# Attention in jobs of four query blocks, with products over up to 512 queries and one buffer for each row of probabilities

## The chip, the cores and the metric

The kernel runs on one core of a Trainium2 chip. The metric is the device time of one execution in microseconds (us), given as the median of several runs. The core has five engines with queues of their own: TensorE (PE in the profile, with its weight loads PEld apart), VectorE (DVE), ScalarE (ACT), GpSimd (POOL), and SyncE (SP), which here only issues DMAs. Each works through its queue in the order of the program; semaphores make one wait for another.

## The reference, cut to what matters

One encoder layer over 1024 tokens and a width of 1024, in float32. Half of the mixer is attention with 8 heads of width 64, in which every query sees itself and the keys ahead of it, and a decay `c` is added to the logits; the other half is a pooling mixer. An output projection, a gated feed-forward layer and a norm follow.

```
for i in range(S // Q_BLOCK):                      # 8 blocks of 128 queries
    q0, q1 = i * Q_BLOCK, (i + 1) * Q_BLOCK
    logits = einsum('bhqd,bhkd->bhqk', qf[:, :, q0:q1], kf[:, :, :q1])
    logits = logits + c[:, :, q0:q1, None] - c[:, :, None, :q1]
    logits = where(s_pos <= t_pos, logits, -inf)
    p = softmax(logits, axis=-1)
    outs.append(einsum('bhqk,bhkd->bhqd', p, vf[:, :, :q1]))
...
x = x + einsum('bse,ed->bsd', concat([attn, pool]), w_out)
x = x + einsum('bsf,fd->bsd', silu(gate) * up, w_down)
```

## The kernel before, in words

Float32 products are made from halves: a matrix is split into a rounded high part and the remainder, and one product becomes three matmuls (`mm3`, lines 157 to 159). The split itself is a copy on ScalarE (line 117) and a subtraction on VectorE or GpSimd (line 118).

The program has three long stages: the norm of the input with the first projections; the attention of the four pairs of heads; then the output projection's rest, the feed-forward layer and the last norm. The change touches the attention alone.

`scores(h, i)` makes a **row of probabilities**, that is the 128 queries of block i of head h against the (i+1)*128 keys that they see. TensorE writes the logits in chunks of up to 512 keys (tile `z`, lines 502 and 503, three PSUM banks in turn). VectorE moves each chunk to the row's tile `p` and takes a minimum (line 505), ScalarE takes the exponent over the whole row (line 511), VectorE the reciprocal of the sum (line 513), and GpSimd scales the row (line 514). Only then may it be transposed.

`turn` transposes a piece of up to four 128x128 blocks of such rows (tile `tp`, line 527, two banks in turn), ScalarE copies it to `th` (line 531) and VectorE makes the remainder `tl` (line 532). `values` multiplies the values of a key block with `th` and `tl` into the bank `po` (line 541), of which there is one. `combine` adds the two halves of `po` (ScalarE's `tmp`, line 552, and VectorE's `at`, line 553) and stores the result to DRAM (tile `mixd`, line 554, an SP queue issue).

A **job** before is a head with a super block `sb` of two query blocks. It has sb+1 pieces; a piece holds two key blocks for the two query blocks, so a product has 256 queries, or 128 where only the second block sees the keys. While a job is turned and multiplied, the rows of the next job are scored. `attend(p, fill, counts)` runs the eight jobs of a pair of heads, and puts steps of other work (`fill`) between: `project` for queries and keys of the next pair (tile `qk`), `project_v23` (tile `v`), and for the last pair the output projection of the chunks that are done (`first_rows` and `second_rows`, tiles `o4`, `o6`, which read the pages `mix` and `wo`). `counts` gives each job its number of fill steps.

This is the order in which the code is written. A scheduler then lays out each engine's queue by when it believes operands to be ready, so that rows of different jobs and fill mix.

Tags set the buffers: the rows 2k and 2k+1 share a tag with two buffers, so there is one buffer for each of a head's eight rows, and a row's logits can be moved by VectorE only when the last transposition of the same row of the head before has run.

After the last job, the last chunk of the mixer's output (`mix3`) is read back from DRAM in two halves (`mix_halves`, lines 749 and 117, 118), while the rest of the fill runs; then `last_row` uses it.

## Time and profile before

| what | value |
|---|---|
| time, median of 3 runs | 1048.54 us (1048.2 to 1049.61) |
| the profiled execution's own time | 1049.96 us |
| its span, first to last instruction | 1048.2 us |
| mean granted TensorE clock | 0.996 |
| first transposition of attention probabilities | 124.5 us after the start |
| last product of probabilities and values | 359.5 us |
| DMA, mean rate over the span | 125 GB/s |

The durations of matmuls in the profile have modelled ends and overlap: a matmul with 512 columns is listed with 0.39 us, yet the next one starts much earlier. How long TensorE is taken by a matmul is therefore read from the start of one to the start of the next. Where such a distance is longer than usual, TensorE stood still, even if the view of waits, which counts from the modelled end, shows less or nothing. For the other engines the listed duration is used.

### The profile page before, as it was taken

To read this page: it belongs to the slowest core of one execution; us is meant where nothing else is said; L and a number is where in the kernel's file an instruction comes from. 1 tells how busy PE (TensorE), PEld (TensorE's weight loads), DVE (VectorE), ACT (ScalarE), POOL (GpSimd) and SP (SyncE) were. 2 spreads that over 40 slices of the span, in tenths; PEclk is the share of its full clock that TensorE was granted. 3 is DMA by queue.
4 is the path that set the end of the run, shared out by engine and by line. 5 is a ranking of instruction groups with operands and counts; after the bars stand their busy time and mean duration, and the time that the engine had idled before them with its cause. 6 is when DMAs were issued, how large, how long until landed. Compare 5 with 4: busy or idle time off the path is not lost.

```text
span 1048.2 us, 14193 instructions
## 1 busy us (share of the span) xinstructions
PE 1031.0 (98%) x5104; PEld 871.5 (83%) x5104; DVE 631.0 (60%) x993; ACT 455.5 (43%) x730; POOL 379.9 (36%) x310
## 2 busy tenths in 40 slices
PE   8999999999999999999999999999999999999996
PEld 7988888998888888888888888888888888888885
DVE  5645466666687569753343434334334689788886
ACT  6434364665556347533333333333233343333345
POOL 4350122114237034267347437437537510000044
PEclk9999999999999999999999999999999999999998
DMA  8114434333733125333234143143146755352424
GB/s 272 47 42 127 106 96 99 83 83 96 258 117 107 53 101 181 91 111 116 85 102 140 61 133 118 61 131 111 63 128 236 248 210 174 119 189 92 155 87 160
DMA packets 109462, 130.73 MB, mean 125 GB/s; under 512 B 8272, under 2 KB 71248, under 8 KB 109392
## 3 DMA queue, kind: packets, MB, share of 16 engines
q1 hardware_dynamic: 97952, 108.71, 33.3%
q10 hardware_dynamic: 11088, 20.45, 5.1%
q8 instruction: 40, 0.66, 0.2%
q0 software_dynamic: 352, 0.66, 0.2%
q14 instruction: 30, 0.25, 0.1%
HBM read 86.81 MB, written 33.03 MB: 114 GB/s over the span
## 4 chain that ended last, share of the span: by engine, by line
PE 92%; DVE 2%; issue 2%; DMA 2%; POOL 1%; ACT 1%; POOLq 0%; SPq 0%; DVEq 0%; ACTq 0%
PE gu_P L158 13%; PE gu_P L159 13%; PE gu_P L157 13%; PE d L158 6%; PE d L157 6%; PE d L159 6%; PE po L541 3%; PE tp L527 3%; PE qk L157 3%; PE qk L158 3%; PE o L157 3%; PE o L158 3%; PE qk L159 3%; PE o L159 2%; PE z L503 1%
## 5 line engine op out<-in xcount | busy, mean ns | idle before, releaser
L118 DVE TENSOR_TENSOR gu_P_l<-s,gu_P_h 128x1024 fp32r<-128x1024 f32 (+1 forms) x48 | 66.3, 1389 | 98.3 <-ACT gu_P_h L117 93.4
L158 PE MATMUL d<-d,d 128*128 128x512 f32 x308 | 119.9, 389 | 0.0
L159 PE MATMUL d<-d,d 128*128 128x512 f32 x308 | 119.9, 389 | 0.0
L514 POOL TENSOR_SCALAR p<-p,rr 128x128 f32<-128x128 f32 (+3 forms) x64 | 47.6, 749 | 182.1 <-DVE rr L513 152.0
L157 PE MATMUL d<-d,d 128*128 128x512 f32 x308 | 108.2, 389 | 0.0
L117 ACT ACTIVATE d<-r_f 128x1536 fp32r<-128x1536 f32 (+1 forms) x28 | 38.7, 1383 | 117.6 <-PE d L158 105.3
L118 DVE TENSOR_TENSOR gu_P_l<-r,gu_P_h 128x1024 fp32r<-128x1024 f32 x32 | 48.5, 1516 | 64.7 <-ACT gu_P_h L117 64.7
L946 POOL TENSOR_TENSOR s<-r 128x1024 f32<-128x1024 f32 x10 | 24.0, 2398 | 162.9 <-DMA r<-in_w_up_dram 103.1
L117 ACT ACTIVATE gu_P_h<-r 128x1024 fp32r<-128x1024 f32 x32 | 33.9, 1061 | 92.0 <-PE gu_P L158 31.6
L158 PEld LDWEIGHTS d<-d,d 128*128 128x128 f32 x308 | 57.8, 188 | 12.1 <-DVE d L118 0.2
L157 PEld LDWEIGHTS d<-d,d 128*128 128x128 f32 x308 | 57.8, 188 | 12.1
L159 PEld LDWEIGHTS d<-d,d 128*128 128x128 f32 x308 | 57.8, 188 | 12.0
L1169 POOL TENSOR_SCALAR sse<-sse 128x1 f32<-128x1 f32 x8 | 5.2, 646 | 158.2 <-ACT junk L1168 158.2
L511 ACT ACTIVATE p<-p,mn 128x128 f32<-128x128 f32 (+3 forms) x64 | 49.4, 773 | 24.8 <-DVE mn L505 22.2
L532 DVE TENSOR_TENSOR tl<-tp,th 128x512 fp32r<-128x512 f32 (+1 forms) x80 | 49.9, 632 | 16.8 <-ACT th L531 16.5
L531 ACT ACTIVATE th<-tp 128x512 fp32r<-128x512 f32 (+1 forms) x80 | 43.2, 552 | 31.6 <-PE tp L527 20.0
L1033 POOL TENSOR_TENSOR h<-h,qh 128x512 f32<-128x512 f32 x33 | 44.4, 1347 | 31.9 <-ACT qh L1031 23.2
L117 ACT ACTIVATE gu_P_h<-s 128x1024 fp32r<-128x1024 f32 (+1 forms) x48 | 47.0, 984 | 19.1 <-PE gu_P L158 12.1
L1030 DVE TENSOR_TENSOR qh<-gu_P,sn_sU 128x512 f32<-128x512 f32 x22 | 15.2, 690 | 61.1 <-POOL h L1033 32.9
L118 DVE TENSOR_TENSOR d<-r_f,d 128x1536 fp32r<-128x1536 f32 (+1 forms) x28 | 45.6, 1628 | 10.3 <-ACT d L117 10.3
L157 PE MATMUL qk<-hTh,h_qk 128*128 128x512 f32 x128 | 50.3, 393 | 0.9 <-ACT th L531 0.9
L158 PE MATMUL qk<-hTl,h_qk 128*128 128x512 f32 x128 | 50.5, 395 | 0.0
(309 smaller groups left out, 3082.0 us busy)
## 6 DMA issues: line engine op xcount, KB each, us to landing
r_f<-hsdP SPq DMA_DIRECT2D x77, 256.0 KB
r_wd<-in_w_down_dram SPq DMA_DIRECT2D x22, 512.0 KB
hsdP<-f ACTq DMA_DIRECT2D x43, 256.0 KB
r<-in_w_gate_dram SPq DMA_DIRECT2D x21, 512.0 KB
r<-in_w_up_dram SPq DMA_DIRECT2D x21, 512.0 KB
s<-hi SPq DMA_DIRECT2D x64, 128.0 KB
hsdP<-h ACTq DMA_DIRECT2D x32, 256.0 KB
x<-in_x_dram SPq DMA_DIRECT2D x8, 512.0 KB
```

The costliest lines, as they stand in the source:

```text
L117: mark["hi"] = nc.scalar.activation(out=hi, in_=src, func=AF.Copy)
L118: return eng.tensor_tensor(out=lo, in0=src, in1=f32(hi), op=ALU.subtract)
L157: nc.tensor.matmul(ps, lh, rh, start=start, stop=False, **kw)
L158: nc.tensor.matmul(ps, lh, rl, start=False, stop=False, **kw)
L159: mark["mm"] = nc.tensor.matmul(ps, ll, rh, start=False, stop=stop, **kw)
L511: nc.scalar.activation(out=pr[:, :n], in_=pr[:, :n], func=AF.Exp, scale=-1.0, bias=mn, accum_out=rs)
L514: nc.gpsimd.tensor_scalar(out=pr[:, :n], in0=pr[:, :n], scalar1=rr, scalar2=1.0, op0=ALU.mult, op1=ALU.mult)
L527: nc.tensor.transpose(tp[:, w : w + P], probs[h, 2 * sb + a][:, s * P : (s + 1) * P], ident)
L531: nc.scalar.activation(out=th[:, :w], in_=tp[:, :w], func=AF.Copy)
L532: nc.vector.tensor_tensor(out=tl[:, :w], in0=tp[:, :w], in1=f32(th[:, :w]), op=ALU.subtract)
L541: mark["pv"] = nc.tensor.matmul(po[:, first * P : 2 * P], vt[p][:, s, j, :], part[:, o : o + wd], start=(s == 0 and part is th), stop=(s = ...
L1033: nc.gpsimd.tensor_tensor(out=h, in0=h, in1=q, op=ALU.mult)
```

## The change

A job is now a head with four query blocks (r0 = 0 or 4), so there are 16 jobs in place of 32. A piece is one key block for all of the job's query blocks that see it; the last two of the four diagonal key blocks that are narrow share a piece as told in `pieces`. A head has ten pieces before and after, with the same 36 transposed blocks. Products now have 512, 384, 256 or 128 queries. All four rows of the next job are scored during a job, and the first four rows of the first head at the start. `combine` runs 16 times over 512 queries in place of 32 times over 256, and `tmp` has one buffer in place of two. Each row of probabilities has a tag and one buffer of its own size. The counts of fill steps of two old jobs are summed; in the last pair they are 29 in place of 27 of 32 steps, so that 3 steps in place of 5 are left behind the last job.

```
-        pr = ap_.tile([P, (2 * (i // 2) + 2) * P], F32, tag=f"pr{i // 2}", bufs=2, name=f"p{h}_{i}")
+        pr = ap_.tile([P, n], F32, tag=f"pr{i}", bufs=1, name=f"p{h}_{i}")
...
+    def pieces(r0):
+
+        return [(s,) for s in range(r0 + 1)] + [(r0 + 1, r0 + 3), (r0 + 2,)]
...
-        for s in (2 * pc, 2 * pc + 1):
-            first = 0 if s <= 2 * sb else 1
+        for s in pieces(r0)[pc]:
+            first = max(0, s - r0)
             spans.append((s, w, first))
-            for a in range(first, 2):
-                nc.tensor.transpose(tp[:, w : w + P], probs[h, 2 * sb + a][:, s * P : (s + 1) * P], ident)
+            for a in range(first, nr):
+                nc.tensor.transpose(tp[:, w : w + P], probs[h, r0 + a][:, s * P : (s + 1) * P], ident)
...
-            wd = (2 - first) * P
+            wd = (nr - first) * P
             for part in (th, tl):
                 mark["pv"] = nc.tensor.matmul(
-                    po[:, first * P : 2 * P], vt[p][:, s, j, :], part[:, o : o + wd],
-                    start=(s == 0 and part is th), stop=(s == 2 * sb + 1 and part is tl),
+                    po[:, first * P : nr * P], vt[p][:, s, j, :], part[:, o : o + wd],
+                    start=(s == 0 and part is th), stop=(s == end and part is tl),
                 )
...
-        tmp = ap_.tile([P, 256], F32, tag="tmp", bufs=2, name=f"tmp{h}_{sb}")
-        at = ap_.tile([P, 256], F32, tag="at", bufs=2, name=f"at{h}_{sb}")
-        nc.scalar.activation(out=tmp[mine, :], in_=po[other, 0:256], func=AF.Copy)
-        nc.vector.tensor_tensor(out=at[mine, :], in0=po[mine, 0:256], in1=tmp[mine, :], op=ALU.add)
-        nc.sync.dma_start(out=mixd[p, mine, sb * 256 : (sb + 1) * 256], in_=at[mine, :])
+        w = nr * P
+        tmp = ap_.tile([P, 512], F32, tag="tmp", bufs=1, name=f"tmp{h}_{r0}")
+        at = ap_.tile([P, 512], F32, tag="at", bufs=2, name=f"at{h}_{r0}")
+        nc.scalar.activation(out=tmp[mine, :w], in_=po[other, :w], func=AF.Copy)
+        nc.vector.tensor_tensor(out=at[mine, :w], in0=po[mine, :w], in1=tmp[mine, :w], op=ALU.add)
+        nc.sync.dma_start(out=mixd[p, mine, r0 * P : r0 * P + w], in_=at[mine, :w])
...
-    jobs = [(h, sb) for h in range(H) for sb in range(NSB)]
+    jobs = [(h, r0, 4) for h in range(H) for r0 in (0, 4)]
...
-    attend(0, project(1), [5, 4, 4, 3, 8, 6, 6, 0])
-    attend(1, both(project(2), project_v23()), [10, 7, 6, 8, 10, 8, 12, 0])
+    attend(0, project(1), [9, 7, 14, 6])
+    attend(1, both(project(2), project_v23()), [17, 14, 18, 12])
...
-    attend(2, project(3, first_chunk), [5, 2, 1, 6, 14, 7, 7, 1])
+    attend(2, project(3, first_chunk), [7, 7, 21, 8])
...
-    attend(3, fill, [3, 3, 4, 4, 4, 4, 3, 2], drain=False)
+    attend(3, fill, [6, 8, 7, 8], drain=False)
```

The order of every queue between the first transposition and the last product changes with it; before and behind that stretch TensorE's queue holds the same rows in the same order. Three places follow. In names like `tp1_0_1`, the first number is the head, the second the job (sb before, r0 now), the third the piece; `z1_7_512` is head 1, row 7, the chunk from key 512; `p1_2` is head 1, row 2.

**Place 1**, TensorE where head 0 ends and head 1 begins. Before, behind the logits of head 1's row 7:

```order
L502 MATMUL z1_7_512_1789<-s1_1_0_1_1131,s1_0_0_1_1023 128x512
L503 MATMUL z1_7_512_1789<-s2_1_0_1_1133,s2_0_0_1_1025 128x512
L502 MATMUL z2_0_0_1831<-s1_1_1_0_1576,s1_0_1_0_1245 128x128
L503 MATMUL z2_0_0_1831<-s2_1_1_0_1578,s2_0_1_0_1247 128x128
L158 MATMUL qk0_2_1_1990<-hTl_106,h_qk0_2_1910 128x512
L541 MATMUL po0_3_1470<-tl0_3_3_1539,v0_174 128x256
L541 MATMUL po0_3_1470<-th0_3_3_1538,v0_174 128x128
L541 MATMUL po0_3_1470<-tl0_3_3_1539,v0_174 128x128
L527 MATMUL tp1_1_0_1648<-ident_62,p1_2_1589 128x128
L527 MATMUL tp1_1_0_1648<-ident_62,p1_3_1606 128x128
```

The same place on TensorE now:

```order
L502 MATMUL z1_7_512_1694<-s1_1_0_1_1131,s1_0_0_1_1023 128x512
L503 MATMUL z1_7_512_1694<-s2_1_0_1_1133,s2_0_0_1_1025 128x512
L546 MATMUL po0_4_1404<-tl0_4_6_1532,v0_174 128x256
L531 MATMUL tp1_0_1_1625<-ident_62,p1_1_1439 128x128
L531 MATMUL tp1_0_1_1625<-ident_62,p1_2_1464 128x128
L531 MATMUL tp1_0_1_1625<-ident_62,p1_3_1492 128x128 x2
L502 MATMUL z2_0_0_1734<-s1_1_1_0_1571,s1_0_1_0_1268 128x128
L503 MATMUL z2_0_0_1734<-s2_1_1_0_1573,s2_0_1_0_1270 128x128
L502 MATMUL z2_1_0_1759<-s1_1_1_0_1571,s1_0_1_0_1268 128x256
L503 MATMUL z2_1_0_1759<-s2_1_1_0_1573,s2_0_1_0_1270 128x256
L531 MATMUL tp1_0_2_1670<-ident_62,p1_2_1464 128x128
L531 MATMUL tp1_0_2_1670<-ident_62,p1_3_1492 128x128
```

Row 7 of head 1 is scored when that head's own first job is being turned, and no `qk` matmul stands between it and its first transposition, which comes 35 matmuls later (`tp1_4_0<-p1_7`); before, its first transposition stood 110 matmuls behind it, 48 of them `qk`.

**Place 2**, ScalarE where head 4 ends, with the pages of the output projection's first chunks (`h_mix6`, `h_wo7`). Before:

```order
L531 ACTIVATE th4_3_3_3125<-tp4_3_3_3121 128x384
L117 ACTIVATE h_mix6_3681<-r_mix6_3564 128x1024
L531 ACTIVATE th5_0_0_3153<-tp5_0_0_3149 128x384
L511 ACTIVATE p5_6_3363,rs5_6_3374<-p5_6_3363,mn5_6_512_3372 128x896
L117 ACTIVATE h_wo7_3741<-r_wo7_3566 128x1024
L552 ACTIVATE tmp4_3_3140<-po4_3_3050 64x256
```

ScalarE there now:

```order
L117 ACTIVATE h_wo5_3417<-r_wo5_3410 128x1024
L535 ACTIVATE th4_4_4_2986<-tp4_4_4_2981 128x512
L535 ACTIVATE th4_4_5_3000<-tp4_4_5_2995 128x512
L511 ACTIVATE p5_4_3054,rs5_4_3065<-p5_4_3054,mn5_4_512_3063 128x640
L535 ACTIVATE th4_4_6_3009<-tp4_4_6_3006 128x256
L117 ACTIVATE h_mix6_3537<-r_mix6_3424 128x1024
L511 ACTIVATE p5_5_3100,rs5_5_3111<-p5_5_3100,mn5_5_512_3109 128x768
L535 ACTIVATE th5_0_0_3036<-tp5_0_0_3031 128x512
L117 ACTIVATE h_wo7_3590<-r_wo7_3426 128x1024
L511 ACTIVATE p5_6_3151,rs5_6_3162<-p5_6_3151,mn5_6_512_3160 128x896
L558 ACTIVATE tmp4_4_3022<-po4_4_2873 64x512
```

One exponent more (`p5_5`) stands between the page `h_mix6` and the copy `tmp` that frees the bank `po` for head 5, and `h_wo5` now stands between the pieces of head 4's long job.

**Place 3**, VectorE where head 5 ends and the second round of output rows (`o6`) begins. Before:

```order
L532 TENSOR_TENSOR tl6_0_0_3536<-tp6_0_0_3531,th6_0_0_3535 128x384
L513 RECIPROCAL rr6_7_3788<-rs6_7_3786 128x1
L553 TENSOR_TENSOR at5_3_3504<-po5_3_3429,tmp5_3_3503 64x256
L695 TENSOR_TENSOR x2_s4_3517<-o4_7_1_3980,x2_s4_3517 128x512
L118 TENSOR_TENSOR hl_wo6_3607<-r_wo6_3562,hl_wo6_3607 128x1024
L532 TENSOR_TENSOR tl6_1_0_3626<-tp6_1_0_3620,th6_1_0_3625 128x512
L513 RECIPROCAL rr7_0_3851<-rs7_0_3849 128x1
L505 ISA p7_2_3969,mn7_2_0_3973<-z7_2_0_3970,wmask_63 128x384
```

VectorE there now:

```order
L118 TENSOR_TENSOR l_wo0_3699<-r_wo0_3542,h_wo0_3698 128x1024
L559 TENSOR_TENSOR at5_4_3358<-po5_4_3235,tmp5_4_3357 64x512
L505 ISA p7_2_3657,mn7_2_0_3661<-z7_2_0_3658,wmask_63 128x384
L505 ISA mn7_2_0_3661 128x1
L505 ISA p7_3_3687,mn7_3_0_3691<-z7_3_0_3688,wmask_63 128x512
L505 ISA mn7_3_0_3691 128x1
L118 TENSOR_TENSOR hl_wo6_3474<-r_wo6_3422,hl_wo6_3474 128x1024
L536 TENSOR_TENSOR tl6_0_1_3469<-tp6_0_1_3463,th6_0_1_3468 128x512
```

The two page subtractions (`l_wo0`, `hl_wo6`) now stand close together, around the addition that frees `po` and the moves of head 7's logits.

More of the change, by code (lines that the diff above doesn't have):

```diff
@@ L533, in turn, with values, combine @@
         return spans, th, tl
-    def values(h, sb, po, piece):
+    def values(h, r0, nr, po, piece):
         p, j = divmod(h, 2)
         spans, th, tl = piece
+        end = pieces(r0)[-1][-1]
         for s, o, first in spans:
-            wd = (2 - first) * P
+            wd = (nr - first) * P
             for part in (th, tl):
                 mark["pv"] = nc.tensor.matmul(
-                    po[:, first * P : 2 * P], vt[p][:, s, j, :], part[:, o : o + wd],
-                    start=(s == 0 and part is th), stop=(s == 2 * sb + 1 and part is tl),
+                    po[:, first * P : nr * P], vt[p][:, s, j, :], part[:, o : o + wd],
+                    start=(s == 0 and part is th), stop=(s == end and part is tl),
                 )
-    def combine(h, sb, po):
+    def combine(h, r0, nr, po):
         p, j = divmod(h, 2)
@@ L549, in combine @@
         other = slice((1 - j) * HD, (2 - j) * HD)
[L550 to L558 removed]
+        w = nr * P
[5 more added lines that the diff above has]
+    jobs = [(h, r0, 4) for h in range(H) for r0 in (0, 4)]
     def job_steps(n):
[L561 removed]
+        h, r0, nr = jobs[n]
         nxt = []
[L563 to L568 removed]
+        for m in jobs[n + 1 : n + 2]:
+            nxt += [(m[0], m[1] + a) for a in range(m[2])]
+        po = bank(f"po{h}_{r0}", "po", 1)
         steps = []
@@ L572, in tr @@
         def tr(pc):
-            held.append(turn(h, sb, pc))
+            held.append(turn(h, r0, nr, pc))
         def pv(pc):
-            values(h, sb, po, held[pc])
-        t_steps = [[lambda pc=pc: tr(pc)] for pc in range(sb + 1)]
-        for pc in range(sb + 1):
-            if pc + 1 <= sb:
+            values(h, r0, nr, po, held[pc])
+        n_pc = len(pieces(r0))
+        t_steps = [[lambda pc=pc: tr(pc)] for pc in range(n_pc)]
+        for pc in range(n_pc):
+            if pc + 1 < n_pc:
                 t_steps[pc + 1].append(lambda pc=pc: pv(pc))
             else:
-                t_steps.append([lambda pc=pc: pv(pc), lambda: combine(h, sb, po)])
+                t_steps.append([lambda pc=pc: pv(pc), lambda: combine(h, r0, nr, po)])
         z_steps = [[lambda t=t: scores(*t)] for t in nxt]
@@ L591, in job_steps @@
         return steps
-    LOOK = 1
-    begun = set()
     def attend(p, fill, counts, drain=True):
         if p == 0:
-            for t in [(0, 0), (0, 1)]:
-                begun.add(t)
+            for t in [(0, a) for a in range(4)]:
                 scores(*t)
@@ L603, in attend @@
         total = sum(counts)
-        for n in range(2 * NSB):
-            steps = job_steps(2 * NSB * p + n)
-            quota = counts[n]
+        for n, quota in enumerate(counts):
+            steps = job_steps(4 * p + n)
             given = 0
```

17 lines of the change are left out of this document (4 added, 13 removed).

## The prediction

> **What bounds the kernel now.** I read the busy shares first, then the stretch of attention by itself, then TensorE's timeline row by row.
>
> ```profile
> PE 1031.0 (98%) x5104; PEld 871.5 (83%) x5104; DVE 631.0 (60%) x993; ACT 455.5 (43%) x730; POOL 379.9 (36%) x310
> 124.00:368.00 244.00, 240.97 (x1472) 211.80 (x1470) 163.81 (x434) 135.64 (x284) 69.88 (x71) 1.00 0.38 109
> ```
>
> The first row is the whole span, the second the stretch that the change reorders (124 to 368 us; length, then busy time of PE, PEld, DVE, ACT, POOL, then clock, DMA share, GB/s). TensorE is listed busy for 241 of 244 us at full clock; the next engine, VectorE, for 164. So the time moves in two ways only: by what TensorE has to issue, and by where it stands still. Ahead of 124 us and behind the last output row its queue is unchanged, so I sum over this stretch alone. That is made against the profiled execution's own 1049.96 us (span 1048.2); the difference is then put on the median, 1048.54 us.
>
> How long a matmul occupies TensorE, from start to start:
>
> ```profile
> 172.13 0.39 PE L159 MATMUL qk<-hTh,l_qk 128*128 128x512 f32 x1
> ...
> 174.86 0.39 PE L159 MATMUL qk<-hTh,l_qk 128*128 128x512 f32 x1
> ```
>
> Twelve intervals of 512-column matmuls in 2.73 us are **0.227 us** each.
>
> ```profile
> 167.14 0.33 PE L502 MATMUL z<-s,s 128*128 128x384 f32 x1
> 167.31 0.34 PE L503 MATMUL z<-s,s 68*128 68x384 f32 x1
> 167.49 0.39 PE L502 MATMUL z<-s,s 128*128 128x512 f32 x1
> ...
> 205.60 0.28 PE L541 MATMUL po<-tl,v 128*128 128x256 f32 x1
> 205.72 0.22 PE L541 MATMUL po<-th,v 128*128 128x128 f32 x1
> 205.78 0.27 PE L541 MATMUL po<-tl,v 128*128 128x128 f32 x1
> 205.89 0.34 PE L158 MATMUL v<-l_v,hTh 128*128 128x256 f32 x1
> ```
>
> Likewise 384 columns take **0.175**, 256 take **0.120**, and a `th`, `tl` pair of 128 together **0.17** (205.72 to 205.89).
>
> **The change part by part.** *Products.* Both kernels push the same 73,728 columns.
>
> ```profile
> L541 PE MATMUL po<-th,v 128*128 128x256 f32 x128 | 34.6, 293 | 0.1
> ```
>
> Before, with `tl` as often as `th`, and 32 pairs of 128: 256 x 0.120 + 32 pairs x 0.17 = 36.2 us. After, counted from the diff for 16 jobs (per head: 12 of 512, 4 of 384, 4 of 256 and 4 of 128 columns): 96 x 0.227 + 32 x 0.175 + 32 x 0.120 + 16 pairs x 0.17 = 21.8 + 5.6 + 3.8 + 2.7 = 33.9 us. **Saved: 2.3 us** (2.0 to 2.7 as the paces are read 0.002 us to either side). 128 matmuls fewer thus save 18 ns each: twice 0.120 is only 13 ns over 0.227. The 288 transpositions stay.
>
> A rule speaks against even that: the Trainium skill, "TensorE: Matmul & The Clock Gate", section "Back-to-back issue gap", gives an isolated warm gap of columns/2.4 GHz plus 2.5 ns. By it, an estimate, fusing pairs saves some 0.3 us in all. The rows above are 11 and 14 ns longer than it for 512 and 256 columns, so here a fixed part near 15 ns is seen, and the trace decides for 2.3.
>
> *Side work.* `combine`:
>
> ```profile
> L552 ACT ACTIVATE tmp<-po 64x256 f32<-64x256 f32 x32 | 12.1, 379 | 20.6 <-PE po L541 20.1
> L553 DVE TENSOR_TENSOR at<-po,tmp 64x256 f32<-64x256 f32 x32 | 13.4, 419 | 10.8 <-ACT tmp L552 10.3
> L531 ACT ACTIVATE th<-tp 128x512 fp32r<-128x512 f32 x48 | 28.0, 594 | 20.5 <-PE po L541 10.6 <-PE tp L527 9.0
> L532 DVE TENSOR_TENSOR tl<-tp,th 128x512 fp32r<-128x512 f32 x48 | 32.4, 686 | 10.2 <-ACT th L531 10.1
> ```
>
> 64 x 512 is not there; it lies between its 64 x 256 form (0.38, 0.42) and the 128 x 512 rows (0.59, 0.69). I take 0.59 and 0.6. ScalarE and VectorE so lose some 3 us of 136 and 164, beside TensorE, worth nothing by itself. There are 15 handovers of `po` in place of 31, each 0.2 to 0.4 us longer; at most of them the order puts at least 1.9 us of matmuls between the last product of a job and the first of the next, which covers 1.2. SP issues 16 stores fewer, of twice the bytes; GpSimd's 64 scalings stay. I cost these at nothing; at a handover without cover it is up to 0.4 us.
>
> *Waits.* Here the order matters. First what TensorE stands still before:
>
> ```profile
> 170.09 0.62 PE L527 MATMUL tp<-ident,p 128*128 128x128 f32 x4
> 171.59 0.47 PE L157 MATMUL qk<-hTh,h_qk 128*128 128x512 f32 x1 [0.88 <-ACT th L531]
> ...
> 286.80 0.39 PE L503 MATMUL z<-s,s 68*128 68x512 f32 x1
> 288.06 0.50 PE L502 MATMUL z<-s,s 128*128 128x512 f32 x1 [0.87 <-DVE mn L505]
> ...
> 352.10 0.52 PE L527 MATMUL tp<-ident,p 128*128 128x128 f32 x3
> 353.24 0.63 PE L527 MATMUL tp<-ident,p 128*128 128x128 f32 x4 [0.62 <-DVE tl L532]
> ...
> 356.73 0.28 PE L541 MATMUL po<-th,v 128*128 128x256 f32 x1
> 357.10 0.38 PE L541 MATMUL po<-tl,v 128*128 128x256 f32 x1
> ...
> 358.24 0.28 PE L541 MATMUL po<-tl,v 128*128 128x256 f32 x1
> 358.63 0.39 PE L541 MATMUL po<-th,v 128*128 128x256 f32 x1
> 359.22 0.39 PE L541 MATMUL po<-tl,v 128*128 128x256 f32 x1 [0.20 <-DVE tl L532]
> ...
> 367.63 0.39 PE L159 MATMUL o<-h_wo,hl_mix 128*128 128x512 f32 x1
> 368.18 0.50 PE L157 MATMUL o<-hl_wo,h_mix 128*128 128x512 f32 x1 [0.16 <-DVE x_s L695]
> ```
>
> Start to start less the pace: 1.50 - 4 x 0.109 (a transposition) = 1.1 us; 1.26 - 0.23 = 1.0; in the tail 0.8 + 0.25 + 0.27 + 0.47 = 1.8; 0.55 - 0.23 = 0.3. **Before: 4.2 us.** Then what stands there after, from the new order with these paces:
>
> Place 1. Row 7 has 35 matmuls (4.8 us) until its transposition.
>
> ```profile
> L505 DVE CUSTOM_DVE_ANT_0 p<-z,wmask 128x512 f32<-128x512 f32 x40 | 27.1, 684 | 10.6 <-PE tp L527 7.6 <-PE z L503 2.9
> ...
> L511 ACT ACTIVATE p<-p,mn 128x1024 f32<-128x1024 f32 x8 | 9.2, 1144 | 2.5 <-DVE mn L505 2.5
> ...
> L511 ACT ACTIVATE p<-p,mn 128x896 f32<-128x896 f32 x8 | 8.3, 1043 | 7.4 <-DVE mn L505 6.1 <-issue 1.3
> ...
> L514 POOL TENSOR_SCALAR p<-p,rr 128x1024 f32<-128x1024 f32 x8 | 9.0, 1125 | 20.7 <-DVE rr L513 11.5 <-DVE at L553 3.3 <-PE tp L527 3.2
> ```
>
> Its chain is a move of 0.68, the exponent 1.14, a reciprocal over one column, estimated at 0.2, and the scaling 1.13: 3.2. ScalarE has `tmp` and two `th` ahead of the exponent (1.7 together), VectorE `at`, two `tl` and two moves ahead of the reciprocal, of which I count 1.3 as not covered: 6.2, a stall of 1.4. Bounds: 0 (queues empty, 3.2 is under 4.8) and 2.5 (all of VectorE's operations in the way). That replaces the 1.1: **+0.3**.
>
> Place 2. The pages are loaded behind the last `qk` matmul, whose queue position keeps them where they were:
>
> ```profile
> 268.04 0.40 PE L159 MATMUL qk<-hTh,l_qk 128*128 128x512 f32 x1
> ...
> 272.50 1.06 ACT L117 ACTIVATE h_wo<-r_wo 128x1024 fp32r<-128x1024 f32 x1 [0.47 <-DMA r_wo<-in_w_out_dram]
> ...
> 282.05 1.06 ACT L117 ACTIVATE h_mix<-r_mix 128x1024 fp32r<-128x1024 f32 x1 [4.19 <-DMA r_mix<-mixd]
> ```
>
> From the last `qk` (ending 268.27) `h_wo5` is copied 5.3 us later (272.50 + 1.06). After, its first user stands 25 matmuls behind that `qk` (13 of 512, 12 transpositions: 4.3 us): a stall of 1.0. `h_mix6` starts 13.8 us behind the `qk`; ScalarE then has, in the order quoted, that page 1.06, the exponent `p5_5` of 768 keys about 0.94 (0.1 below the 896 form, as that lies below the 1024 form), `th5_0_0` 0.59, `h_wo7` 1.06, `p5_6` 1.04 and `tmp` 0.6, and VectorE `at` 0.6: `po` is free at 19.7. TensorE reaches head 5's first product 17.0 us of matmuls later plus the stall of 1.0: 18.0, a stall of 1.7. Together 2.7 for 1.0: **+1.7**, bounds -1.0 (pages 2.7 us earlier) to +4.7 (3 us later), since each us of landing is a us here.
>
> Place 3. VectorE, in the order quoted:
>
> ```profile
> L118 DVE TENSOR_TENSOR l_wo<-r_wo,h_wo 128x1024 fp32r<-128x1024 f32 x3 | 4.5, 1493 | 0.5 <-ACT h_wo L117 0.4
> L118 DVE TENSOR_TENSOR hl_wo<-r_wo,hl_wo 128x1024 fp32r<-128x1024 f32 x1 | 1.6, 1554 | 0.0
> ```
>
> Behind the end of `z7_1` on TensorE come its move (0.4), `l_wo0` 1.5, `at` 0.6, two moves of logits (0.6 and 0.7) and `hl_wo6` 1.55: 5.3 us until TensorE may use the low half of that page. TensorE has matmuls for 2.9 us in that time (8 of 512 and 2 of 384 columns for logits and `o6`, three products of `po6_0` and a short piece of logits). **+2.4**, bounds 0 (the page's subtraction done ahead of the logits) and 3; before, this place shows no stall.
>
> Tail. The last job turns one piece after another with 1.1 us of matmuls between a piece's transposition and the use of its remainder; `th` and `tl` take 0.59 + 0.69 and two handovers near 0.1: 1.4. Three times 0.3 and a last one of 0.6 are 1.5. Then
>
> ```profile
> 360.68 2.70 DMA mixd<-at
> 363.52 2.62 DMA r_mix<-mixd
> ```
>
> the store and the load, with a copy and a subtraction of 128 x 512 (the price of `th` and `tl`, 1.3), run beside 27 matmuls of fill (three steps, 6.1 us) where five steps (45, 10.2 us) stood, so about 0.9 comes to light. 2.4 for 2.1: **+0.3**, bounds -1 and +1.5.
>
> **Sum:** -2.3 + 0.3 + 1.7 + 2.4 + 0.3 = **+2.4 us**: 1052.4 in the profiled execution's own terms, **1050.9** on the median.
>
> **The rivals.** *A: the waits are covered.* Rows elsewhere are scored a whole four-block job ahead, and if pages and logits arrive as TensorE wants them, only the saving is left: 1048.54 - 2.3 = 1046.2; if the two stalls of before at places 1 and 2 (2.1) go as well, 1044.1. For it: ScalarE and VectorE are idle for 108 and 80 of the 244 us. Against: idle engines do not help a queue that stands behind one late page, as the 4.19 us wait at 282.05 shows.
>
> *B: slower by the page on ScalarE.* If `r_mix6` lands 3 us later than I place it, because the stores of twice the size and the logits of four rows share the queues, every operation behind `h_mix6` on ScalarE waits too: 1050.9 + 3 = 1053.9, 1052 to 1057. It decides from about 1.5 us on. For it: 4.19 us of waiting are there already.
>
> *C: TensorE goes by columns alone.* Then nothing is saved: 1053.2. The 13 ns above speak against it. That the change does nothing of what it says is excluded: the order shows 96 products of 512 columns.
>
> **How the numbers follow.** Forecast (1048.8 to 1052.6) 0.48, half of it on either side of 1050.6; A 0.27, of it 0.22 below 1046.4; B 0.18; C 0.03; 0.04 other mixtures near no change. What a measurement of this kernel can tell from no change is about 0.2%, 2.1 us: faster than 1046.4 has 0.22, within 0.24 + 0.05 + 0.04 = 0.33, slower than 1050.6 0.24 + 0.18 + 0.03 = 0.45. The range runs from the middle of A to the middle of B, 1044.8 to 1054.5, which leaves out about 0.15.
>
> **What would show it.** In the profile after: starts of 512-column products 0.227 apart; a gap on TensorE ahead of `tp` behind row 7 of head 1 near 1.4; one ahead of the first `o` with `h_wo` behind the last `qk` (1.0) and one at head 5's first `po` (1.7), released by VectorE's `at`; one near 2.4 at the first `o` of the second round; no gaps over 0.6 in the tail. The forecast is wrong if the gaps of the stretch sum to under 6 or over 12 us (4.2 before, 8.9 by the sum), or if 512 columns do not keep their pace with `v` as weights.

## The result, and the profile after

| kernel | median, us | lowest to highest | time against the kernel before, with 95% interval |
|---|---|---|---|
| before | 1048.36 | 1047.54 to 1049.66 | 1 |
| after | 1050.59 | 1048.61 to 1051.97 | 1.0021 [1.0014, 1.0027] |

The change costs 2.2 us; 1050.9 was predicted. The profiled execution of after took 1051.61 us (span 1049.8), that of before 1049.96. Since single executions of after lie 3.4 us apart, both kernels were profiled a second time later (1049.53 and 1047.34 us; experiments 9 and 12 below), and I read all four.

First the busy shares of after, from its page:

```profile
PE 1030.0 (98%) x4976; PEld 863.0 (82%) x4976; DVE 631.2 (60%) x977; ACT 451.7 (43%) x714; POOL 381.6 (36%) x310
```

Then the window of attention, 124 to 368 us (length, busy time of PE, PEld, DVE, ACT and POOL, clock, DMA share, GB/s):

```profile
124.00:368.00 244.00, 239.21 (x1335) 204.18 (x1335) 161.57 (x416) 130.65 (x266) 71.09 (x71) 0.99 0.37 107
```

The program has 128 matmuls fewer, VectorE and ScalarE some 2 and 5 us less to do in the stretch, and TensorE is still listed busy for nearly all of it. Against the rows of before, TensorE is busy for 1.8 us less in a window of the same length, and the clock is 0.99: it stands still longer, and part of the time it runs slower. TensorE's timeline of after says where. **Place 1**, behind row 7 of head 1:

```profile
166.22 0.41 PE L531 MATMUL tp<-ident,p 128*128 128x128 f32 x2
166.80 0.44 PE L502 MATMUL z<-s,s 128*128 128x384 f32 x1 [0.17 <-DVE mn L505]
...
170.59 0.40 PE L503 MATMUL z<-s,s 68*128 68x512 f32 x1
171.38 0.44 PE L531 MATMUL tp<-ident,p 128*128 128x128 f32 x2 [0.39 <-POOL p L514]
```

Start to start less the pace, that is 0.58 - 0.22 = 0.36 and 0.79 - 0.23 = 0.56: 0.9 us where 1.1 stood before, ended by a move of logits and by GpSimd's scaling of the row. **Place 2**, with the first user of `h_wo5`, TensorE's rows without a gap in them, then ScalarE's copies of pages, then three windows of 3.41 us, cut where the granted clock changes (columns as above):

```profile
270.51 0.48 PE L546 MATMUL po<-th,v 128*128 128x512 f32 x1
272.53 0.96 PE L157 MATMUL o<-h_wo,h_mix 128*128 128x512 f32 x2 [1.54 <-ACT h_wo L117]
273.29 0.63 PE L546 MATMUL po<-tl,v 128*128 128x512 f32 x1
273.71 1.05 PE L531 MATMUL tp<-ident,p 128*128 128x128 f32 x4
274.42 0.78 PE L546 MATMUL po<-th,v 128*128 128x512 f32 x1
274.99 0.63 PE L158 MATMUL o<-l_wo,h_mix 128*128 128x512 f32 x1
275.42 0.63 PE L159 MATMUL o<-h_wo,l_mix 128*128 128x512 f32 x1
275.85 0.59 PE L158 MATMUL o<-l_wo,h_mix 128*128 128x512 f32 x1
276.27 0.40 PE L159 MATMUL o<-h_wo,l_mix 128*128 128x512 f32 x1
```

```profile
271.42 1.06 ACT L117 ACTIVATE h_wo<-r_wo 128x1024 fp32r<-128x1024 f32 x1 [1.97 <-DMA r_wo<-in_w_out_dram]
...
279.05 1.06 ACT L117 ACTIVATE h_mix<-r_mix 128x1024 fp32r<-128x1024 f32 x1 [1.20 <-DMA r_mix<-mixd]
```

```profile
269.44:272.86 3.42, 1.81 (x9) 1.08 (x8) 1.28 (x3) 1.45 (x3) 0.00 (x0) 1.00 1.01 255
272.86:276.27 3.41, 3.41 (x11) 2.72 (x10) 3.15 (x9) 1.53 (x4) 0.00 (x0) 0.50 1.01 297
276.27:279.68 3.41, 3.41 (x19) 2.93 (x18) 3.10 (x9) 1.01 (x2) 0.81 (x1) 1.00 1.03 423
```

The stall is 2.02 - 0.23 = 1.8 us. Behind it the granted clock is 0.50, and 512-column matmuls start 0.43 us apart (275.42 to 275.85). From 272.53 to 276.27 stand seven of them and four transpositions, 7 x 0.23 + 4 x 0.109 = 2.05 us at full clock; they took 3.74, so **the slow clock cost another 1.7 us**. The busy share hides this: a matmul at half the clock counts as busy twice as long. The clock is at half its rate for the whole window of 3.41 us from 272.86 to 276.27, which is worth the same 1.7 us. ScalarE's copy of the page waited for its transfer, at a DMA share of 1.00 all through.

**Place 3**, TensorE, then VectorE and GpSimd:

```profile
315.35 0.73 PE L157 MATMUL o<-hl_wo,h_mix 128*128 128x512 f32 x2
317.68 0.47 PE L546 MATMUL po<-th,v 128*128 128x512 f32 x1 [1.60 <-DVE at L559]
...
319.13 0.40 PE L503 MATMUL z<-s,s 68*128 68x512 f32 x1
319.93 0.50 PE L158 MATMUL o<-hl_wo,h_mix 128*128 128x512 f32 x1 [0.40 <-DVE hl_wo L118]
```

```profile
314.15 2.66 DVE L118 TENSOR_TENSOR l_wo<-r_wo,h_wo 128x1024 fp32r<-128x1024 f32 x1
316.84 0.69 DVE L559 TENSOR_TENSOR at<-po,tmp 64x512 f32<-64x512 f32 x1
...
318.66 1.22 DVE L118 TENSOR_TENSOR hl_wo<-r_wo,hl_wo 128x1024 fp32r<-128x1024 f32 x1
```

```profile
313.33 2.39 POOL L118 TENSOR_TENSOR hl_mix<-r_mix,hl_mix 128x1024 fp32r<-128x1024 f32 x1
```

The stalls are 2.33 - 2 x 0.23 = 1.9 and 0.80 - 0.23 = 0.6, with about 0.6 in smaller distances around them: 3.1 us where before had none. `at` stands on VectorE behind `l_wo0`. That subtraction began while GpSimd's was running and took 2.66 us: GpSimd's ended at 315.72, and `l_wo0` 1.1 us after that. The same kind of subtraction took 1.22 us at 318.66, with GpSimd idle.

**The tail.** The last job's turning and the wait for `mix3`:

```profile
359.94 0.50 PE L546 MATMUL po<-th,v 128*128 128x512 f32 x1
360.66 0.50 PE L546 MATMUL po<-tl,v 128*128 128x512 f32 x1 [0.23 <-DVE tl L536]
...
372.85 0.39 PE L159 MATMUL o<-h_wo,mix_l 128*128 128x512 f32 x1
373.79 0.50 PE L157 MATMUL o<-h_wo,h_mix 128*128 128x512 f32 x1 [0.55 <-DVE x_s L692]
```

0.72 - 0.23 = 0.5 is one of two such gaps; with 0.25, 0.2 and the last, 0.94 - 0.23 = 0.7, the tail sums to 2.1, as before.

How far this is typical shows in the second profile of each. The table has the stretch from the first transposition of probabilities to the first product of the feed-forward layer (`gu_P`), and the distances on TensorE beyond the pace of each form, summed over all its rows there (those over 0.06 us):

| profile | first transposition | first `gu_P` | stretch, us | stalls in it, us |
|---|---|---|---|---|
| before | 124.49 | 408.35 | 283.86 | 13.3 |
| before, again | 124.43 | 405.62 | 281.19 | 10.6 |
| after | 123.83 | 410.55 | 286.72 | 17.7 |
| after, again | 124.25 | 408.47 | 284.22 | 15.2 |

Either pair of profiles says the same: the stretch is 2.9 and 3.0 us longer, of which stalls are 4.4 and 4.6 more; the products therefore give back 1.5 or 1.6. About 6.4 us in each of the four sums is not standing still: the last transposition of a run is followed by the next matmul after 0.03 us instead of 0.109, and that matmul is then 0.08 us longer. Without this the sums are about 6.8, 4.1, 11.3 and 8.9 us.

The whole executions differ by less than the stretch, 1.65 and 2.19 us. Behind the first `gu_P` both profiles of after are 0.6 us shorter than those of before; ahead of the first transposition they are 0.7 and 0.2 us shorter (the first profile of before has half the clock there, from 11.43 to 14.84 us, and the first of after has not).

Within each kernel the stretch of one execution differs from that of the other by 2.5 us or more, most of it at place 2. In the second profile of after, with the same queues:

```profile
270.89 0.48 PE L546 MATMUL po<-th,v 128*128 128x512 f32 x1
271.82 0.74 PE L157 MATMUL o<-h_wo,h_mix 128*128 128x512 f32 x2 [0.44 <-ACT h_wo L117]
...
313.47 0.73 PE L157 MATMUL o<-hl_wo,h_mix 128*128 128x512 f32 x2
315.80 0.47 PE L546 MATMUL po<-th,v 128*128 128x512 f32 x1 [1.59 <-DVE at L559]
```

```profile
272.00:274.00 2.00, 2.00 (x11) 1.63 (x12) 2.00 (x4) 0.85 (x2) 0.00 (x0) 1.00 1.07 258
```

Place 2 is 0.93 - 0.23 = 0.7 us here and no slow clock follows; place 3 is the same 1.9 to the hundredth. The second profile of before doesn't stand still between the two chunks of logits where its first stood for 1.0 us:

```profile
285.68 0.39 PE L503 MATMUL z<-s,s 68*128 68x512 f32 x1
285.92 0.40 PE L502 MATMUL z<-s,s 128*128 128x512 f32 x1
```

In the two profiles of after the copy of `wo5` begins 5.2 and 4.2 us behind the end of the last `qk` matmul. So place 2 goes by when transfers land, which varies; place 3 goes by the order of queues, which doesn't.

### The profile page after: what moved, and what is told of

The parts are those of the page before. It is cut to its first block, busy times and chain, and to the rows that moved or that the text cites. A ratio compares the mean times of both kernels' runs of the same rounds, so it can differ in the third digit from the quotient of the medians.

```text
span 1049.8 us, 13811 instructions
## 1 busy us (share of the span) xinstructions
PE 1030.0 (98%) x4976; PEld 863.0 (82%) x4976; DVE 631.2 (60%) x977; ACT 451.7 (43%) x714; POOL 381.6 (36%) x310
## 4 chain that ended last, share of the span: by engine, by line
PE 92%; DVE 3%; DMA 2%; ACT 1%; issue 1%; POOL 1%; POOLq 0%; SPq 0%; DVEq 0%; ACTq 0%
PE gu_P L158 13%; PE gu_P L159 13%; PE gu_P L157 13%; PE d L158 7%; PE d L157 7%; PE d L159 7%; PE po L546 3%; PE qk L157 3%; PE qk L158 3%; PE qk L159 3%; PE tp L531 3%; PE o L157 2%; PE o L158 2%; PE o L159 2%; PE z L503 1%; PE z L502 1%
## 5 line engine op out<-in xcount | busy, mean ns | idle before, releaser
L1027 DVE TENSOR_TENSOR qh<-gu_P,sn_sU 128x512 f32<-128x512 f32 x22 | 15.2, 690 | 62.3 <-POOL h L1030 44.9
```

## The experiments

The theory: the change saves some 2 us of products and pays for them with waits at places 2 and 3. The rivals: the time goes with the products themselves, or with the tail, or with whatever order the scheduler makes. The shift is each kernel's ratio less that of after (1.0021), times 1048 us.

| | kernel | median, us | ratio to before, 95% interval | shift from after, us |
|---|---|---|---|---|
| 1 | page `wo5` loaded a pair earlier | 1053.85 | 1.0052 [1.0040, 1.0064] | +3.2 |
| 2 | `l_wo0` on GpSimd | 1050.07 | 1.0014 [1.0006, 1.0023] | -0.7 |
| 3 | 1 and 2 together | 1052.27 | 1.0045 [1.0033, 1.0057] | +2.5 |
| 4 | products of at most 256 queries | 1049.38 | 1.0012 [1.0003, 1.0021] | -0.9 |
| 5 | row loads issued behind the pages | 1048.97 | 1.0008 [0.9998, 1.0017] | -1.4 |
| 6 | buffers of `wo6` and `wo0` swapped | 1047.85 | 0.9994 [0.9986, 1.0003] | -2.8 |
| 7 | low half of `mix0` on VectorE | 1050.35 | 1.0021 [1.0012, 1.0030] | 0 |
| 8 | two more steps left for the tail | 1052.46 | 1.0038 [1.0026, 1.0051] | +1.8 |
| 9 | after, unaltered | 1050.40 | 1.0022 [1.0013, 1.0030] | +0.1 |
| 10 | 5 and 6 together | 1049.17 | 1.0009 [1.0000, 1.0018] | -1.3 |
| 11 | 6 in the kernel before | 1054.13 | 1.0059 [1.0047, 1.0072] | |
| 12 | before, unaltered | 1048.12 | 1.0001 [0.9992, 1.0010] | |

### 1. The page `wo5` a pair earlier

```
 # in first_chunk, behind the load of mix5
+        raw_page("wo", NPAIR + 1, wpool, "wr")
 # in first_rows
-        raw_page("wo", 5, op, "ol")
```

> The changed kernel, with the raw page wo5 loaded ahead of the last qk matmul, into a buffer that is free by then, instead of behind it. Theory: the wait for this page (1.7 us on TensorE at 270.5 us) and the stretch at half clock behind it (3.4 us, worth some 1.7 us) are what place 2 costs, so the time falls by 1.7 to 3.5 us, to 1047.1 to 1048.9, and the profile shows the granted clock at 1.00 from 260 to 290 us. Rival 1 (the loss lies in the handovers of po and in the shorter look-ahead of rows, not in the pages): no change, 1050.6. Rival 2 (another page, r_mix6, becomes the next late one at head 5's first product, as the prediction had it): it falls by less than 1 us, to about 1050, with a stall of 1 to 2 us there.

It became slower by 3.2 us: a miss. The page is no longer late, but its copy now stands on ScalarE right behind that of `mix5`, ahead of `th`, and TensorE waits there instead. ScalarE's timeline, then TensorE's:

```profile
267.09 1.05 ACT L117 ACTIVATE h_mix<-r_mix 128x1024 fp32r<-128x1024 f32 x1
268.04 1.04 ACT L117 ACTIVATE h_wo<-r_wo 128x1024 fp32r<-128x1024 f32 x1
268.99 1.07 ACT L535 ACTIVATE th<-tp 128x512 fp32r<-128x512 f32 x2
```

```profile
267.76 0.60 PE L531 MATMUL tp<-ident,p 128*128 128x128 f32 x4
269.63 0.50 PE L546 MATMUL po<-th,v 128*128 128x512 f32 x1 [1.27 <-ACT th L535]
...
271.19 0.50 PE L157 MATMUL o<-h_wo,hl_mix 128*128 128x512 f32 x1 [1.06 <-DVE lo L449]
```

Two copies of 1.05 us keep `th` for 2.1; the stalls are 1.87 - 4 x 0.109 = 1.4 and 1.56 - 0.23 = 1.3, the second behind the page's subtractions on VectorE, and the slow clock follows (0.50 from 272.36 to 275.78). A further stall of 1.2 us stands at 280 us, and place 3 is followed by half the clock too (320.15 to 323.56). So the wait of place 2 wasn't had away by an early page alone: with the page late, ScalarE was free for `th`.

### 2. `l_wo0` on GpSimd

```
-            ("mix", 7, ST1, nc.gpsimd), ("wo", 0, ST0, nc.vector), ("mix", 0, VB, nc.gpsimd),
+            ("mix", 7, ST1, nc.gpsimd), ("wo", 0, ST0, nc.gpsimd), ("mix", 0, VB, nc.gpsimd),
```

> The changed kernel, with the low half of page wo0 computed on GpSimd instead of VectorE. Theory: at place 3 TensorE waits for the addition at (2.66 us of l_wo0 stand ahead of it on VectorE, beside a 2.39 us subtraction on GpSimd); without l_wo0 the addition comes 2.7 us earlier and the 1.76 us stall ahead of head 6's first product goes, so the time falls by 1 to 2 us, to 1048.6 to 1049.6. VectorE's subtraction hl_wo6 then meets GpSimd's, and should take over 1.5 us instead of 1.22 us if two subtractions hinder one another. Rival (VectorE's moves of logits or the page hl_wo6 are late next): under 0.5 us is gained, and the stall stands some matmuls later.

0.7 us less, with intervals that overlap. `at` now comes early and the stall at head 6's first product is gone, but the subtraction of `hl_wo6` on VectorE begins while the one moved to GpSimd runs. VectorE's row, then GpSimd's:

```profile
313.79 3.05 DVE L118 TENSOR_TENSOR hl_wo<-r_wo,hl_wo 128x1024 fp32r<-128x1024 f32 x1
```

```profile
313.37 2.38 POOL L118 TENSOR_TENSOR l_wo<-r_wo,h_wo 128x1024 fp32r<-128x1024 f32 x1
```

`hl_wo6` takes 3.05 us instead of 1.22, ending 1.1 us behind GpSimd's end at 315.75; TensorE waits 2.3 us for it, and the slow clock follows (0.50 from 317.10 to 320.51). That the wait at `at` is VectorE's queue is shown; the time was not won back, since the wait moved.

### 3. Both together

> Both edits together. Theory: the two places are apart by 45 us and add up: 3 to 5 us less than the changed kernel, 1045.6 to 1047.6, so below the kernel before (1048.4) by 0.8 to 2.8 us, about the 2.3 us that the wider products save. Rival (the loss is spread over handovers): within 1 us of 1050.6. If one stall only moves into the other place, the sum is under 2 us.

1052.27: slower by what the two shifts add up to (3.2 - 0.7 = 2.5), and far from the 3 to 5 us less of the theory. The losses of 1 remain.

### 4. Products of at most 256 queries

All of the change stays, but each product of 512 or 384 queries is issued in pieces of at most 256, so TensorE has as many matmuls as before.

```
-                mark["pv"] = nc.tensor.matmul(
-                    po[:, first * P : nr * P], vt[p][:, s, j, :], part[:, o : o + wd],
...
+                for c in range(0, wd, 256):
+                    n = min(256, wd - c)
+                    mark["pv"] = nc.tensor.matmul(
+                        po[:, first * P + c : first * P + c + n], vt[p][:, s, j, :], part[:, o + c : o + c + n],
...
```

> The changed kernel with every product of more than 256 queries issued as two, so that the products have the widths of before (256 and 128), in jobs of four query blocks. Theory: the wider products save 2.3 us, so this kernel takes 2.3 us more than the changed one, 1052.9 (1052.4 to 1053.4), less or more by what the scheduler's order changes with it. Rival C (columns alone count): the same as the changed one, 1050.6.

It is no slower than after, rather 0.9 us faster, with overlapping intervals; the forecast of 1052.9 missed. That isn't because products of 512 save nothing: the scheduler made another order, whose stalls sum to 13.1 us where the second profile of after has 15.2. Its stretch is 283.56 us, 0.7 shorter with 2.1 us fewer stalls, so what TensorE issues takes 1.4 us more (2.1 if the 0.08 us behind transpositions is counted apart). The wide products save that much, and the order they bring costs more.

### 5. Row loads issued behind the pages

The first two loads of rows of `x` (`x2_load`), which stood among those of the pages, are issued behind `mix6`; each load waits for the issue of the one ahead of it. (Only the issue order of transfers changes.)

```
...
         raw_page("wo", 5, op, "ol")
-        x2_load(ORDER[0])
...
-        x2_load(ORDER[1])
         for kind, c, tag in (("wo", 6, "oh"), ("mix", 6, "ml"), ("wo", 7, "mh"), ("mix", 7, "ol")):
-            raw_page(kind, c, op, tag)
+            with tc.issue_after(mark["raw"].ins):
+                raw_page(kind, c, op, tag)
+                if c == 6 and kind == "mix":
+                    x2_load(ORDER[0])
+                    x2_load(ORDER[1])
...
```

> The changed kernel with the loads of the input rows (x_r, x_s) issued behind the pages wo5, wo6 and mix6, which they shared the DMA engines with; TensorE's queue between the last qk and the first product with h_wo5 is the same, 25 matmuls. Theory: r_wo5 has some 0.9 MB in flight beside it in place of 1.4 MB and lands 1 to 2 us earlier, so the stall at place 2 shrinks from 1.7 us to under 0.7 and no stretch at half clock follows: the time falls by 1 to 3.5 us, to 1047.1 to 1049.6. Rival 1 (place 2 costs little in most executions, since the stall was 0.6 us in another run with the same queue there): it falls by under 1 us. Rival 2 (the pages behind it come later and TensorE waits at head 5's first product): no change or slower.

1.4 us less, and executions only 1.5 us apart instead of 3.4. TensorE at place 2:

```profile
270.71 0.47 PE L546 MATMUL po<-th,v 128*128 128x512 f32 x1
272.08 0.73 PE L157 MATMUL o<-h_wo,h_mix 128*128 128x512 f32 x2 [0.89 <-ACT h_wo L117]
```

The stall is still 1.37 - 0.23 = 1.1 us, as the copy of `wo5` starts at 270.97, between those of the two profiles of after (271.42 and 270.71). `h_mix6` is copied at 275.10, 3 to 4 us earlier than in these (279.05 and 278.33). No slow clock follows, and place 3 keeps 2.5 us. So loads of rows do stand in the way of a page, but of `mix6` rather than of `wo5`. That the executions lie closer together would fit a slow clock that is missing in all of them; one profile doesn't show that.

### 6. The buffers of `wo6` and `wo0` swapped

`h_wo6` goes to a buffer that is free at once (`ST0`), `h_wo0` to the one (`VC`) that `v` leaves last. The work is the same, but `hl_wo6` can be made earlier and `l_wo0` later.

```
-            ("wo", 6, VC, nc.vector), ("mix", 6, ST0, nc.gpsimd), ("wo", 7, W, nc.vector),
-            ("mix", 7, ST1, nc.gpsimd), ("wo", 0, ST0, nc.vector), ("mix", 0, VB, nc.gpsimd),
+            ("wo", 6, ST0, nc.vector), ("mix", 6, ST0, nc.gpsimd), ("wo", 7, W, nc.vector),
+            ("mix", 7, ST1, nc.gpsimd), ("wo", 0, VC, nc.vector), ("mix", 0, VB, nc.gpsimd),
```

> The changed kernel with the pages wo6 and wo0 in one another's buffers: the page in the buffer that only comes free with head 5's last product is then the one that the second round of output rows reads last, and VectorE has the addition at ahead of a subtraction instead of behind it. Theory: the stalls of place 3 (1.8 us ahead of head 6's first product, 0.6 us ahead of the low half of wo6, 0.7 us at logits) go to under 1 us together: the time falls by 1.5 to 2.5 us, to 1048.1 to 1049.1. Rival (GpSimd, with two subtractions of pages in a row ahead of the scaling of row 7 of head 6, is late next): under 0.5 us is gained and the stall stands at a transposition of head 6.

2.8 us less than after, the intervals apart: as fast as before, and the best order of the change found. VectorE at place 3:

```profile
311.59 0.69 DVE L559 TENSOR_TENSOR at<-po,tmp 64x512 f32<-64x512 f32 x1
...
312.80 1.34 DVE L118 TENSOR_TENSOR hl_wo<-r_wo,hl_wo 128x1024 fp32r<-128x1024 f32 x1
```

`at` now stands ahead of the subtraction, as the theory of place 3 wants. GpSimd's row:

```profile
313.02 3.37 POOL L118 TENSOR_TENSOR l_mix<-r_mix,h_mix 128x1024 fp32r<-128x1024 f32 x1
```

Here VectorE's subtraction began first and nearly kept its time, and GpSimd's is the longer one, at which TensorE doesn't wait. What is left there is 0.3 + 0.7 us of stalls in place of 3.1; place 2 has 0.6, and two new stalls, 0.7 and 0.4, stand at 387 to 391 us.

### 7. The low half of `mix0` on VectorE

The subtraction that ran on GpSimd beside `l_wo0` goes to VectorE.

```
-            ("mix", 7, ST1, nc.gpsimd), ("wo", 0, ST0, nc.vector), ("mix", 0, VB, nc.gpsimd),
+            ("mix", 7, ST1, nc.gpsimd), ("wo", 0, ST0, nc.vector), ("mix", 0, VB, nc.vector),
```

> The changed kernel with the low half of page mix0 computed on VectorE instead of GpSimd, so that no subtraction of GpSimd runs beside those of VectorE at place 3. Theory (two subtractions of 128 x 1024 on both engines hinder one another): l_wo0 takes 1.2 us in place of 2.66 and hl_wo6 1.2, although VectorE has one more subtraction of 1.2 us to do; the time stays within 1 us of the changed kernel's 1050.6. Rival (l_wo0 is long for a reason of its own, its page's buffer or the DMA beside it): it takes over 2 us again, and the time rises by about 1.2 us to 1051.8.

The time is after's. VectorE at place 3:

```profile
313.83 1.22 DVE L118 TENSOR_TENSOR l_wo<-r_wo,h_wo 128x1024 fp32r<-128x1024 f32 x1
...
315.80 1.23 DVE L118 TENSOR_TENSOR hl_wo<-r_wo,hl_wo 128x1024 fp32r<-128x1024 f32 x1
```

Without GpSimd beside it the subtraction takes 1.22 us in place of 2.66, which shows what had slowed it. But VectorE has more in its queue: the stalls at place 3 are still 1.6 + 0.7 + 0.5, the first at logits behind the subtraction that was moved (1.74 us at 310.94), and one of 1.1 us stands at the last job's first product.

### 8. Two more steps left for the tail

```
-    attend(3, fill, [6, 8, 7, 8], drain=False)
+    attend(3, fill, [6, 8, 7, 6], drain=False)
```

> The changed kernel with 27 steps of fill in the last pair of heads in place of 29, as before, so that 5 steps in place of 3 stand behind the last job. Theory: the store, load and splits of the last chunk are covered, and the 0.7 us ahead of the last output rows goes; the gaps between the last job's pieces (1.3 us) get no larger, since those pieces had no fill between them anyway: the time falls by 0.3 to 0.7 us, to 1049.9 to 1050.3. Rival (the two steps are missing between the pieces of the last job): the time rises by 0.5 to 1.5 us.

1.8 us more, the rival's case and a little above its range. `mix3` is better covered (its gap 0.4 in place of 0.7 us), but what was taken out of the last job had covered its `at`. TensorE there:

```profile
353.34 0.71 PE L531 MATMUL tp<-ident,p 128*128 128x128 f32 x5
355.00 0.47 PE L546 MATMUL po<-th,v 128*128 128x512 f32 x1 [0.95 <-DVE at L559]
```

1.66 - 5 x 0.109 = 1.1 us, which after doesn't have. The change's choice of 3 steps for the tail is thus better than before's 5.

### 9. After, unaltered

> The changed kernel itself once more, unaltered, for a second profile. Theory: the order and so the places of the stalls are fixed (place 3 again 2.5 to 3.1 us), but the wait for page wo5 at place 2 varies with the transfer (0.5 to 1.7 us in the kernels with the same queue there), and the stretch at half clock behind a stall of 1.7 us is there in some executions only; the median is 1050.6 again (1050.0 to 1051.0). Rival (each stall of over 1.5 us is always followed by half clock): the stall of place 3 shows it too.

1050.40, as the theory has it, and the second profile that was read with the result. The rival is refuted: the stall of 1.9 us at place 3 left the clock at 1.00.

### 10. 5 and 6 together

> The changed kernel with both edits that helped: rows loaded behind the pages, and wo6 and wo0 in one another's buffers. Theory (the gains add): 1050.6 - 1.6 - 2.7 = 1046.3, that is 2 us below the kernel before. Rival: the two edits together give another order, in which head 5's first product stands 13.8 us of matmuls behind the last qk in place of 16.9, so TensorE waits there for ScalarE's page wo7 and tmp for 1 us or more, and the time is that of the swap alone, 1047.9, or above.

-1.3 us, less than 6 alone, with intervals that just overlap: the rival's case. The scheduler's order is another one again, and place 2 has three stalls (0.6, 0.7 and 0.75 us) at 271 to 277 us, where 6 has one of 0.6.

### 11. The swap in the kernel before

> The kernel before, with the pages wo6 and wo0 in one another's buffers: the control for that edit. Theory: the kernel before has no stall at place 3 that the swap could take away, so it stays within 1 us of 1048.3, and what the swap gained in the changed kernel was the price of the new order there. Rival (the swap is an improvement by itself): 2 to 3 us less, 1045.3 to 1046.3.

6.0 us slower than the unaltered kernel before, measured beside it (1048.13). Theory and rival both missed: the same swap that mends the order of after spoils that of before, with stalls of 1.0, 1.3 and 0.4 us at 281 to 285 and one of 0.9 at 392.6. The swap is no improvement in itself; it suits one order.

### 12. Before, unaltered

> The kernel before once more, unaltered, for a second profile, since one execution of each kernel need not be the typical one. From the first transposition of probabilities to the first gate product its profile took 283.86 us, the changed kernel's two profiles 286.72 and 284.22, while the medians differ by 2.2. Theory: the stalls at 170, 352 to 360 and 368 us follow from the order and come again within 0.2 us, and the ones at 284 to 288 us (0.5 and 1.06), which follow a page's transfer, vary, so that a typical execution takes 282.4 to 283.4 us for this stretch. Rival: it takes 283.9 us again, and the difference of the medians comes from the stretches at half clock alone.

1048.12, and the second profile of before read above. Its stretch is 281.19 us, below the theory's 282.4 to 283.4: the stalls at 170 us and between the last job's pieces came again, those at 284 to 288 us are gone altogether, and so is the one at 368.

## Why the prediction held, point by point

The total came out right, 2.2 us slower for 2.4; several of its terms did not.

| term | predicted | measured in the first pair of profiles | in the second pair |
|---|---|---|---|
| products | -2.3 | -1.6 | -1.5 |
| place 1 | +0.3 | -0.2 | -0.2 |
| place 2 | +1.7 | +2.0 | +0.7 |
| place 3 | +2.4 | +3.1 | +3.1 |
| tail | +0.3 | 0 | +0.2 |
| not foreseen: the last output row | 0 | +0.6 | +0.6 |
| what is left over, many distances under 0.3 us | 0 | -1.0 | +0.1 |
| stretch | +2.4 | +2.9 | +3.0 |
| behind the stretch | 0 | -0.6 | -0.6 |

- **Products** were mis-sized. The pace of 512 columns was read in a stream of `qk` matmuls (0.227). Of the 96 such products in the second profile of after, the 72 that no stall and no transposition ahead lengthens have a mean distance of 0.2324 us to the next matmul; 231 of 256 columns in before have 0.119. That is 2 x 0.119 - 0.2324 = 5.6 ns a pair in place of 13; with the narrow ones, 256 x 0.119 + 32 x 0.173 = 36.0 against 96 x 0.2324 + 32 x 0.178 + 32 x 0.1185 + 16 x 0.17 = 34.5 us: **1.5 us**, below the predicted range of 2.0 to 2.7. Only 0.5 of it comes from products of 512 columns; 0.9 comes from those of 384, each of which stands for one of 256 and one of 128. The difference of stretches and stalls (1.6, 1.5) and experiment 4 (1.4 to 2.1) agree, though they rest on the same paces. One number in the prediction's comparison is off besides: 0.120 for 256 columns is 11 ns above the 0.109 of the formula that it quotes, not 14. Rival C, that TensorE goes by columns alone, is refuted, though a pair's 5.6 ns is nearer to its 0 than to the forecast's 13.
- **Place 1** was too dear. The row did come late for its transposition, released by GpSimd's scaling as said, but by 0.56 us and not 1.4. Its chain was right: from the end of its last logits (165.16) to its transposition (171.38) are 6.2 us, with the reciprocal held up for 1.3 on VectorE. But TensorE took 5.7 us for the 35 matmuls between, in place of 4.8, as it had stood 0.4 us at other logits (166.80) and smaller distances added up.
- **Place 2** was right in its place and releaser for `h_wo5`, and wrong in two ways. The 1.0 us there is 1.8 in one execution, 0.7 in another; the page's landing decides, at a DMA share of about 1.00. The 1.7 us at head 5's first product did not come: `r_mix6` was copied 12.9 us behind the last `qk` (11.8 in the second profile), not 13.8, and in the first profile TensorE came later by what it lost at half the clock. That loss, 1.7 us, was not in the forecast at all. The stall of before that I subtracted (1.0; another 0.5 stood ahead of it) is absent from its second profile, so the base was one execution's accident.
- **Place 3** was right in its mechanism, `l_wo0` ahead of `at` and `hl_wo6` behind it on VectorE. I priced both subtractions near 1.5, a mean over before's three for `l_wo` (the one there at 311.68 takes 1.23); they were 2.66 and 1.22, by whether GpSimd was subtracting. I expected the wait at the low half of `wo6`; most of it (1.9 of 3.1) stands at head 6's first product, whose bank `at` frees. Experiments 2, 6 and 7 show the queue as the cause: 2 and 6 take `l_wo0` from ahead of `at`, and that stall goes; 7 leaves it there at 1.22 us in place of 2.66, and 0.7 us remain. Each has new stalls elsewhere; those of 6 are the smallest (0.7 and 0.4). The stall is the same in both profiles of after and in neither of before, so **it is the change's cost**, larger than the products' gain.
- **The tail** is as long as before: the gaps of turning are 0.5, 0.5, 0.25 and 0.2 where I had three of 0.3 and one of 0.6, and the wait for `mix3` is 0.7 where I had 0.9. (The narrow key blocks share a piece as `pieces` has it, the first with the third and the second by itself, and not as the text on the change says.) Experiment 8 shows that the cost of more fill behind the job would have been higher.
- **Unforeseen**: the last output row starts 0.47 us (second profile 0.49) behind the last of the eight transpositions ahead of it, where both profiles of before have 0.03, and the first two matmuls of the next stage lie 0.40 apart instead of 0.26. The profile names VectorE's addition of an earlier output (`x_s`) as the releaser. Why it is late there was not tried. After gains as much, 0.6 us, behind the stretch; that the one is the other's return is not shown. By summing over the stretch alone the prediction left the second out.
- **The signs** that the prediction named: the gaps of the stretch sum to 11.3 and 8.9 us, within its 6 to 12 (8.9 was forecast). One gap of the tail, 0.7 ahead of the last output rows, is over its 0.6, and the pace of 512 columns with `v` as weights is 0.232 in place of 0.227.
- **Rivals**: A (waits covered) is refuted in this order, since place 3 stands in both profiles; experiment 6, the best order found, stays 1.7 us above its 1046.2. B (the page on ScalarE) did not decide: that page came earlier than I had it, and place 2's cost was `wo5`'s.

The net was right by luck, because errors offset: place 1, head 5's first product and the tail were too dear, and against that the saving was too large by 0.8, place 3 too cheap by 0.7, and a slow clock and the last output row were not counted; the stretch came out 0.5 longer than forecast, which the 0.6 behind it hid. What stays open is which phase of place 2 a given execution meets.

## What to carry to other kernels

Fewer and wider instructions on the engine that bounds shorten its queue and give the scheduler another order; here 1.5 us of issue was saved and the stalls around a page's subtraction took 3.1, so read the order for what now stands ahead of the operation that frees a bank. Where stalls hang on transfers, one profile is one draw: profile both kernels twice before a stall is put into a sum, and price an elementwise operation by what runs beside it. Mend an order by giving the page that is read first the buffer that is free first (2.8 us here), and expect that the same edit can do harm in another order (6.0 us).
